# Taking over rooms for a latent attention stage one by one, with the last two projections side by side

## The chip, the cores and the metric

The kernel runs on one core of one Trainium2 chip. The metric is device time of one execution in microseconds (us), lower being better: here the median of three runs. TensorE does the matrix products, VectorE and ScalarE take results out of its banks (PSUM) and split or scale them, GpSimd (POOL) does some sums, and SyncE (SP) issues most transfers between memory and the on-chip buffer (SBUF), in the order in which they stand in its queue.

## The reference

One layer of a streaming encoder over 592 token rows: 16 learned meta rows, 512 prompt frames and 64 sample frames (with 128 cached rows in front of the latter). Everything is float32.

```python
z = rmsnorm(x, g) @ w_in                      # 8 differential heads (q, k, v), query latent 512, key latent 256, rotary key 64
cq = rmsnorm(cq_part, mla_q_norm_g)           # 4 blocks of 128: the "query latents"
qm = cq @ w_uq                                # per head 128 plain and 64 rotary columns
qm = concat(qm_plain, rope(qm_rot, pos))
ckv = rmsnorm(ckv_part, mla_kv_norm_g); krope = rope(kr_part, pos)
km, vm = expand_latent(ckv, w_ukv)            # per head 128 key and 128 value columns
sm = (qn . km + qr . krope) * MLA_SCALE       # 8 latent heads; softmax, times vm
x = x + concat(o_d, o_m) @ w_out              # o_d: 8 differential ("old") heads, o_m: 8 latent heads
x = x + (silu(h @ w_gate) * (h @ w_up)) @ w_down
```

`rope` turns the first and second half of 64 columns: `concat(x1*cos - x2*sin, x1*sin + x2*cos)`. The outputs hold the new keys, values, latents and rotated keys too.

## The kernel before

Activations lie transposed, 128 features on the partitions and the tokens along the row: 592 columns (`T`), 576 without the meta rows (`TQ`), 720 with the cached rows (`TP`). A float32 product is made of three products of rounded parts: an operand is split into a high part (ScalarE, `AF.Copy`) and a low part (VectorE, the subtract), and `mm3` (line 200) multiplies wh by xh, wh by xl and wl by xh, each in two halves of the columns.

The first stage (the block from line 333) holds x split into 16 rooms of high and low parts (`xh`, `xl`, pool `xp`). `projections()` (662) makes the 24 projections of the differential heads, whose attention (`diff_attend`) runs interleaved with it, and then seven more of 128 columns each: the key latents 4 and 5, the rotary key 6 (64 columns, loaded twice to fill 128: `dup`), and the query latents 0 to 3. Each is 16 pieces of x by six matmuls. After the rotary key, `key_latent_norm()` takes its squares' sum with `sum_squares()` (306), whose matmuls against ones run in full float32. Each differential head's output is stored to `mspill[h]`.

The second stage (from line 721) has pools of its own, so it begins when the first stage is over: it loads the eight old heads back from `mspill` (line 729, seven through POOL's queue), cos, sin, the rotation matrix, the cached rows and both masks. `latents()` (790) turns the rotary key (`rope`, 777: a matmul with the matrix `rot`, then a product with sin and one with cos), transposes the cached rows, splits the latents, and takes the query latents' norm. `latent_rows()` (821) transposes the latents back for the outputs. `heads()` (981) does the eight latent heads: `rotary_queries` for each pair of heads, `queries_keys`, `pair_values`, and `latent_attend`, which stores to `mspill[8 + h]`. `mix_out()` (851) multiplies the old heads with the first half of w_out, 16 outputs of 8 by 6 matmuls, each output (`xo`) added to x and stored to `x1spill`.

TensorE's program order is made by `Streams` (50 to 97): generators with a rank each, and a clock that the matmuls advance; the ready one of lowest rank goes on. `mix_out` has rank 30, so its products fill in where nothing else is ready. On the other engines the order follows from the same run, with a scheduler's changes.

The third stage (from line 1148) does the second half of the out-projection: pool `ma` has three rooms `x`, into which the eight latent heads are loaded and split:

```python
m = ma.tile([P, TQ], F32, name="x", tag="x", bufs=3)
load(m, mspill[8 + h])
```

Then the FFN follows (lines 1138 and 1142), by far the longest part. A pool's first tiles wait for all that used the same ground before.

## Time and profile before

| | us |
|---|---|
| median of 3 runs | 2452.48 (2449.06 to 2455.5) |
| the profiled execution | 2450.92 |
| its span in the profile | 2449.1 |
| TensorE busy (matmul) | 2391.8, 98% |
| VectorE busy | 1778.9, 73% |
| ScalarE busy | 1161.0, 47% |
| GpSimd busy | 714.6, 29% |

The busy shares are averages over the three stages. TensorE's share says only that waits are short in all; where they are and what ends them must be looked for in the stretches around the change, which lie between 430 and 840 us.

### The profile page before, as it was taken

The page shows a single profiled execution, that of the slowest core. Times are in us where ns is not written, and L with a number is a line of the kernel's source. Part 1 is how long each engine was busy: PE and PEld are TensorE (multiplying, and loading weights), DVE is VectorE, ACT ScalarE, POOL GpSimd, SP SyncE. Part 2 cuts the span into 40 slices and gives each one's busy share as a digit, 9 for nine tenths or more (in the row PEclk, how much of TensorE's full clock was granted, in tenths as well). Part 3 has the DMA queues.
Part 4 walks back from the last instruction along what each step waited for, and adds up shares of the span by engine and source line. Part 5 has one row for each costly group of instructions (what it writes and reads, how often), then busy time and mean ns, then how long its engine had stood idle before and what let it go on. Part 6 is the DMA issues. An engine that isn't in the chain of part 4 may idle for free.

```text
span 2449.1 us, 44580 instructions
## 1 busy us (share of the span) xinstructions
PE 2391.8 (98%) x17607; PEld 2350.9 (96%) x17607; DVE 1778.9 (73%) x2815; ACT 1161.0 (47%) x2204; POOL 714.6 (29%) x553
## 2 busy tenths in 40 slices
PE   8999999989999999999999999999999999999998
PEld 7999999978999899999999999999999999999998
DVE  5665566556555588777888788888887988887874
ACT  5544544343444455445555554555554433333445
POOL 0000000000000144645645445445454322222223
PEclk9999999989999999999999999999999999999999
DMA  8432323243322553334434443443344875654332
GB/s 246 135 92 83 82 82 98 73 129 110 105 87 72 181 170 127 122 104 157 137 130 146 142 154 116 152 157 127 135 150 163 287 237 175 225 164 162 106 116 83
DMA packets 334864, 338.02 MB, mean 138 GB/s; under 512 B 24208, under 2 KB 278039, under 8 KB 334655
## 3 DMA queue, kind: packets, MB, share of 16 engines
q1 hardware_dynamic: 334094, 333.11, 42.7%
q8 instruction: 138, 2.26, 0.4%
q0 software_dynamic: 560, 2.06, 0.2%
q14 instruction: 72, 0.58, 0.1%
HBM read 265.20 MB, written 72.61 MB: 138 GB/s over the span
## 4 chain that ended last, share of the span: by engine, by line
PE 52%; DVE 1%; DMA 0%; issue 0%; POOL 0%; ACT 0%; DVEq 0%; POOLq 0%; SPq 0%
PE m L1138 33%; PE m L1142 17%; PE m L204 2%; DVE wl L124 0%; PE m L1521 0%; DMA raw<-in_ffn_w_down 0%; DVE b L124 0%; DMA b<-sumspill 0%; POOL ws L1107 0%; DVE ws L124 0%; PE m L1535 0%; DVE y L124 0%; ACT wh L124 0%; POOL b L1508 0%; DVE c L124 0%
## 5 line engine op out<-in xcount | busy, mean ns | idle before, releaser
L1138 PE MATMUL m<-b,wh 128*128 128x288 f32 x7168 | 1048.0, 295 | 5.8 <-ACT wh L124 2.9
L1138 PEld LDWEIGHTS m<-b,wh 128*128 128x128 f32 x7168 | 983.6, 188 | 8.5 <-issue 4.6
L1142 PE MATMUL m<-b,wl 128*128 128x288 f32 x3584 | 580.2, 297 | 1.7 <-DVE wl L124 1.5
L1107 POOL TENSOR_TENSOR ws<-raw 128x512 f32<-128x512 f32 (+1 forms) x258 | 373.4, 1457 | 543.4 <-DVE wl L124 263.0
L1142 PEld LDWEIGHTS m<-b,wl 128*128 128x128 f32 x3584 | 514.0, 189 | 3.0 <-DVE wl L124 3.0
L124 ACT ACTIVATE wh<-ws 128x512 fp32r<-128x512 f32 (+1 forms) x340 | 283.3, 846 | 389.9 <-PE m L1138 251.5
L124 DVE TENSOR_TENSOR wl<-ws,wh 128x512 fp32r<-128x512 f32 (+1 forms) x340 | 386.9, 1149 | 89.6 <-ACT wh L124 89.6
L124 ACT ACTIVATE wh<-raw 128x512 fp32r<-128x512 f32 x387 | 227.4, 620 | 288.1 <-PE m L1138 258.0
L124 DVE TENSOR_TENSOR wl<-raw,wh 128x512 fp32r<-128x512 f32 x387 | 358.4, 952 | 7.3 <-ACT wh L124 6.8
L107 PE MATMUL ps<-xh,wh 128*128 128x296 f32 (+1 forms) x960 | 218.8, 309 | 1.4 <-ACT wh L124 1.4
L107 PE MATMUL ps<-xl,wh 128*128 128x296 f32 (+1 forms) x960 | 210.3, 300 | 1.5 <-DVE xl L124 1.5
L107 PE MATMUL ps<-xh,wl 128*128 128x296 f32 (+1 forms) x960 | 209.3, 299 | 0.7 <-DVE wl L124 0.6
L124 DVE TENSOR_TENSOR y<-y,m 128x288 f32<-128x288 f32 x312 | 140.1, 451 | 88.3 <-PE m L1142 68.0
L124 DVE TENSOR_TENSOR ws<-ws,raw 128x512 f32<-128x512 f32 (+1 forms) x129 | 110.3, 857 | 80.3 <-POOL ws L1107 78.5
L107 PEld LDWEIGHTS ps<-xh,wh 128*128 128x128 f32 x960 | 156.6, 191 | 5.2 <-ACT wh L124 2.1
L107 PEld LDWEIGHTS ps<-xl,wh 128*128 128x128 f32 x960 | 157.2, 191 | 2.2 <-DVE xl L124 2.2
L107 PEld LDWEIGHTS ps<-xh,wl 128*128 128x128 f32 x960 | 156.9, 191 | 1.4 <-DVE wl L124 1.4
L124 DVE TENSOR_TENSOR wl<-wr,wh 128x1024 fp32r<-128x1024 f32 (+1 forms) x110 | 117.1, 1065 | 43.4 <-ACT wh L124 42.1
L124 ACT ACTIVATE wh<-wr 128x1024 fp32r<-128x1024 f32 (+1 forms) x110 | 102.4, 932 | 69.5 <-PE ps L107 41.8
L1326 POOL TENSOR_TENSOR c<-c,rb 128x576 f32<-128x576 f32 x44 | 70.7, 1609 | 168.2 <-ACT c L124 168.2
L591 POOL MEMSET bias<- 64x64 f32 x8 | 1.2, 145 | 373.6 <-DMA bias<-tsk 321.7
L124 ACT ACTIVATE parts<-c 128x1 fp32r<-128x1 f32 x252 | 81.2, 322 | 37.5 <-DVE c L124 31.8
(354 smaller groups left out, 3110.7 us busy)
## 6 DMA issues: line engine op xcount, KB each, us to landing
raw<-in_ffn_w_gate SPq DMA_DIRECT2D x44, 1024.0 KB, 5.9
raw<-in_ffn_w_up SPq DMA_DIRECT2D x44, 1024.0 KB, 6.1
raw<-in_ffn_w_down SPq DMA_DIRECT2D x39, 1024.0 KB, 5.6
partspill<-parts SPq DMA_DIRECT2D x126, 288.0 KB, 2.1
b<-partspill SPq DMA_DIRECT2D x126, 288.0 KB, 6.0
wr<-in_w_in SPq DMA_DIRECT2D x60, 512.0 KB, 4.0
wr<-in_w_out SPq DMA_DIRECT2D x16, 512.0 KB, 4.0
wr<-in_w_out SPq DMA_DIRECT2D x32, 256.0 KB, 3.3
```

The source lines that it names most:

```text
L107: self.tc.keep_in_program_order(self.pe.matmul(out, lhsT, rhs, start=start, stop=stop))
L124: ins = issue(*args, **kwargs)
L204: PE.matmul(outs[i], w, x[i], start=start and p == 0, stop=stop and p == 2)
L591: G.memset(bias[0:64, 464:528], -BIG)
L1107: engine.tensor_tensor(w[:, k:k + m, :], pick(xs), pick(ys), op=op)
L1138: PE.matmul(banks[p], wh[:, k, :], x, start=first and new and k == 0 and x is hi, stop=False, skip_group_check=not new)
L1142: PE.matmul(banks[p], wl[:, k, :], hi, start=False, stop=last and k == n - 1, skip_group_check=not new)
L1326: G.tensor_tensor(g[:, f, :], g[:, f, :], rb2, op=ALU.mult)
```

## The change

The second stage loses its own pools: its tiles go into rooms that the first stage gives up one after the other.

- The last two query latents (2 and 3) are projected side by side, from weights of 4 by 256 columns, so that each piece of x is used for both and then released (`release(kc)`). Rooms 0 to 6 take the old heads 0 to 6 (loaded by SP and split at once), room 7 the last one, which is split from its own tile and no longer stored; room 8 and 9 the head weights (`mw`), 10 cos and sin, 11 the norm and the turned key (later the heads' output `o32`), 12 and 13 the rotary queries with their mask, 14 and 15 the plain queries. The other tiles go into rooms of keys and values (`kv`).
- `rope` has no matmul: four VectorE instructions of 32 partitions multiply each quarter with its sign and with sin into its partner quarter.
- The rotary key is projected with high and low part of the weights side by side in one 128-column operand (`project_stacked`): four matmuls for each piece of x in place of six.
- `sum_squares` adds the squares on GpSimd and multiplies their sum with ones once: two matmuls for four; for the query latents two for eight.
- Both masks are copied early inside memory; the cached rows are loaded in the first stage.
- `mix_out` and `heads` are in the same run of `Streams` as the projections.

```diff
+    def project_stacked(ps, wsrc, xs):
...
+            split(w[:, :, 0:DH], w[:, :, DH:P], wr)
...
+                for j, x in enumerate(xs[kc]):
+                    for i, xi in enumerate(halves(x)):
+                        PE.matmul(ps[:, i, 0:n], w[:, k, :], xi, start=kc + j == 0, stop=kc + j == KC)
...
     def sum_squares(...)
+            if total is None:
+                total = sq
+            else:
+                G.tensor_tensor(total, total, sq, op=ALU.add)
...
+            if h < H - 1:
+                store(mspill[h], o32)
+            else:
+                yield [released[h]]
+                mixh[h], mixl[h] = (x_room(h, w, f"mx{w}{h}")[:, 0:TQ] for w in "hl")
+                split(mixh[h], mixl[h], o32)
...
+            ps = [pjt(), pjt()]
+            for g in range(4):
+                wh, wl = weights(w_in[g * 4 * P:(g + 1) * 4 * P, off:off + 2 * P].rearrange(
+                    "(k p) c -> p k c", p=P), 4, 2 * P)
+                for k in range(4):
+                    kc = 4 * g + k
+                    for j in range(2):
+                        c = slice(j * P, (j + 1) * P)
+                        mm3([ps[j][:, 0, 0:QH], ps[j][:, 1, 0:QH]], wh[:, k, c], wl[:, k, c],
+                            halves(xsq[kc][0]), halves(xsq[kc][1]), kc == 0, kc == KC - 1)
+                        yield 0
+                    release(kc)
...
+        def release(kc):
+            released[kc]["done"] = True
+            if kc < H - 1:
+                mixh[kc], mixl[kc] = (x_room(kc, w, f"mx{w}{kc}")[:, 0:TQ] for w in "hl")
+                load(f32(mixl[kc]), mspill[kc])
+                S.activation(mixh[kc], f32(mixl[kc]), AF.Copy)
+                V.tensor_tensor(mixl[kc], f32(mixl[kc]), f32(mixh[kc]), op=ALU.subtract)
+            elif kc == 10:
+                for w, name, src in (("h", "cos", c_cos), ("l", "sin", c_sin)):
+                    at_x[name] = x_room(kc, w, name, F32)
+                    load(at_x[name], src)
...
         def rope(dst, z):
-            for i in range(2):
-                PE.matmul(pr[:, i, 0:w], rot, z[:, i * w:(i + 1) * w], start=True, stop=True)
-            V.tensor_tensor(hv(t, n), ev(pr, w), hv(sin[:, c], n), op=ALU.mult)
+            for a in range(0, P, 32):
+                b = a ^ 32
+                V.scalar_tensor_tensor(t[b:b + 32, :], z[a:a + 32, :], sign[a:a + 32, :], at_x["sin"][a:a + 32, c],
+                                       op0=ALU.mult, op1=ALU.mult)
...
-            o32 = aq[0].tile([P, TQ], F32, name="o32", bufs=1)
+            o32 = x_room(11, "l", "o32", F32)[:, 0:TQ]
```

What moves shows in the order of the instructions. The first place is TensorE's program behind the last projection matmul (`ps<-xh,wl`; mxh and mxl are an old head's parts, wh and wl weights). Before:

```order
L107 MATMUL ps<-xh_108,wl 128x288 x2
L107 MATMUL pr<-zl_5306,rot 128x296 [waits DMAHW1_49,DVE_49,PE_49]
L107 MATMUL pr<-zl_5306,rot 128x296
L111 MATMUL pkr<-ident,rn 128x128 [waits DMAHW3_49,DMAHW2_49,DMAHW4_49,DMAHW1_49,DMAHW5_49,DMAHW0_49,DMAHW6_49,DVE_49,DMAHW7_49,Activation_49,Pool_49]
L111 MATMUL pkr<-ident,cn 128x128 [waits DMAHW0_49]
L111 MATMUL pkr<-ident,cn 128x128
L107 MATMUL ps<-mxh_5966,wh 128x288 [waits DVE_49,Activation_49]
L107 MATMUL ps<-mxh_5966,wh 128x288
```

With the change, behind nine such rows of the first three old heads (cqh is a query latent's high part, mw a head's weights, sqs the summed squares):

```order
L107 MATMUL ps<-mxh_5693,wl 128x288 x2
L111 MATMUL pkr<-ident,cache 128x128 [waits DMAHW1_49]
L111 MATMUL pkr<-ident,cache 128x128
L111 MATMUL pkr<-ident,cache 128x128 [waits DMAHW3_49,DMAHW2_49]
L107 MATMUL ps<-cqh_5444,mw 128x288 [waits DVE_49]
L107 MATMUL ps<-cqh_5444,mw 128x288
L107 MATMUL ps<-cql_5445,mw 128x288 x2
L107 MATMUL ps<-cqh_5444,mw 128x288 x2
L107 MATMUL ps<-cqh_5622,mw 128x288 x2
L107 MATMUL ps<-cql_5623,mw 128x288 x2
L107 MATMUL ps<-cqh_5622,mw 128x288 x2
L107 MATMUL pq<-sqs,ones 128x288 [waits Pool_49]
```

The rotation and the transposes of the cached rows no longer stand first; three products of old heads do (the first row here is the last of them), then the transposes, then the first head's query projection with the norm's sum inside it.

The second place is VectorE's queue, some 15 instructions behind the evacuation of the last two projections, with the change (xo is an output of the mix, `zq` the first rotary query, `v` and `rsq` the norm's steps):

```order
L124 TENSOR_SCALAR v<-pq 128x576 [waits PE_49,Pool_49]
L124 TENSOR_TENSOR kr<-kr,t 128x592 [waits DVE_49]
L124 TENSOR_TENSOR wl<-wr,wh 128x1024 [waits DMAHW4_49]
L124 TENSOR_TENSOR v<-v,rsq 128x576 [waits DVE_49,Activation_49]
L124 TENSOR_TENSOR rkl_6004<-kr,rkh 64x592 [waits Activation_49]
L124 TENSOR_TENSOR rkl_6005<-kr,rkh 64x592
L124 SCALAR_TENSOR_TENSOR v<-v,rsq 128x576 [waits DVE_49]
L124 TENSOR_TENSOR xo<-xo,ps 128x576 [waits DMAHW4_49,PE_49]
L124 SCALAR_TENSOR_TENSOR rsq<-v,rsq 128x576 [waits DVE_49]
L124 TENSOR_TENSOR mw<-mw 128x512 [waits DMAHW3_49,DMAHW2_49,DMAHW1_49]
L124 SCALAR_TENSOR_TENSOR zq<-ps,rsq 128x576 [waits DVE_49,Pool_49]
L124 TENSOR_TENSOR wl<-wr,wh 128x1024 [waits DMAHW2_49,Activation_49]
```

The four quarters of `t<-zl,sign,sin` (the rotary key) stand just ahead of these rows, those of zq just behind `wl`, and the evacuation of xo between the steps of the norm.

The third place is SP's queue at the end of the latent heads (x: the third stage's rooms; o: a head's output; numbers are the buffers'). Before:

```order
L124 DMA x1spill<-xo 128x576 [waits DMAHW7_49,DVE_49]
L124 DMA x<-mspill 128x576 [waits DMAHW2_49,DMAHW1_49,DMAHW3_49,PE_49,Pool_49]
L124 DMA x<-mspill 128x576 x2
L124 DMA wr<-in_w_out 128x4x128 x2
L124 DMA x<-mspill 128x576 [waits DMAHW3_49,DMAHW0_49,DVE_49]
L124 DMA raw<-in_ffn_w_gate 128x8x256
L124 DMA mspill<-o_9116 128x576 [waits Activation_49]
L124 DMA x<-mspill 128x576 [waits DMAHW4_49,DVE_49]
```

With the change:

```order
L124 DMA mspill<-o_8785 128x576 [waits DMAHW0_49,Activation_49]
L124 DMA x1spill<-xo 128x576 [waits DMAHW6_49,DMAHW1_49,DVE_49]
L124 DMA mspill<-o_9043 128x576 [waits Activation_49]
L124 DMA x<-mspill 128x576 [waits DMAHW2_49,DMAHW0_49,DMAHW3_49,PE_49,Pool_49]
L124 DMA x<-mspill 128x576 x2
L124 DMA wr<-in_w_out 128x4x128
L124 DMA wr<-in_w_out 128x4x128 [waits DMAHW7_49]
L124 DMA x<-mspill 128x576 [waits DMAHW3_49,DVE_49]
```

The store of the last head's output stood behind the first loads of x and of wr; now it stands ahead of all of them. The room of that output lies on ground that the third stage's rooms get.

## Rows read from the trace of the kernel before

**Rows 1.** The table of stretches: us, each engine's busy us and instructions, clock, DMA share, GB/s

```profile
430.00:534.60 104.60, 104.46 (x758) 101.28 (x756) 53.50 (x109) 37.20 (x70) 0.14 (x1) 1.00 0.27 73
534.60:553.00 18.40, 7.71 (x29) 6.24 (x30) 13.70 (x23) 11.37 (x21) 5.32 (x8) 0.63 0.89 286
...
840.00:2449.00 1609.00, 1591.33 (x11935) 1585.20 (x11934) 1288.77 (x1824) 779.19 (x1420) 696.31 (x509) 1.00 0.46 152
```

**Rows 2.** What TensorE waited for, 430 to 830: total us, times, longest

```profile
PE pkr L111 <- DMA kmsk<-c_kmask: 8.1, 1, 8.1
PE pr L107 <- DMA rot<-c_rot: 2.4, 1, 2.4
PE tp L111 <- DVE pk0l L124: 2.0, 2, 1.4
```

**Rows 3.** Timeline of TensorE at the end of the projections: start, us, instruction [idle before]

```profile
534.13 0.42 PE L107 MATMUL ps<-xh,wl 128*128 128x288 f32 x2
536.96 1.79 PE L107 MATMUL pr<-zl,rot 128*128 128x296 f32 x4 [2.41 <-DMA rot<-c_rot]
546.84 0.45 PE L111 MATMUL pkr<-ident,rn 128*128 128x128 f32 x1 [8.09 <-DMA kmsk<-c_kmask]
```

**Rows 4.** Timeline of TensorE, the first latent score

```profile
583.05 0.23 PE L107 MATMUL sp<-kmh,qnh 128*128 128x144 f32 x1
```

**Rows 5.** Timeline of TensorE at the end of the latent heads

```profile
822.51 0.40 PE L107 MATMUL po<-p5h,vl 80*128 80x64 f32 x1
823.27 0.82 PE L204 MATMUL m<-mh,wh 128*128 128x288 f32 x2 [0.36 <-issue]
...
833.05 0.42 PE L204 MATMUL m<-mh,wh 128*128 128x288 f32 x2
```

**Rows 6.** Timeline of TensorE: key projection pairs, a float32 sum

```profile
455.46 0.43 PE L107 MATMUL ps<-xh,wh 128*128 128x296 f32 x2
455.73 0.43 PE L107 MATMUL ps<-xl,wh 128*128 128x296 f32 x2
...
554.03 1.13 PE L107 MATMUL ps<-sq,ones 128*128 128x288 f32 x4
```

**Rows 7.** Instruction groups of VectorE, 430 to 815: busy us, mean ns, idle before

```profile
L124 DVE TENSOR_TENSOR xo<-xo,ps 128x576 f32<-128x576 f32 x16 | 12.0, 752 | 4.6 <-PE ps L107 4.3
...
L124 DVE COPY nn<-pn 128x320 f32<-128x320 f32 x4 | 1.9, 484 | 0.5 <-PE pn L111 0.5
```

**Rows 8.** Instruction groups of GpSimd, 430 to 815

```profile
L786 POOL TENSOR_TENSOR zr<-zq,cos 128x576 f32<-128x576 f32 x4 | 6.6, 1657 | 183.1 <-DVE zq L124 183.1
```

**Rows 9.** Table of stretches, around the two places

```profile
546.80:552.00 5.20, 5.16 (x21) 4.82 (x21) 4.75 (x11) 3.96 (x9) 0.00 (x0) 0.58 1.07 361
820.00:828.00 8.00, 6.96 (x31) 6.60 (x31) 3.71 (x7) 3.29 (x7) 0.00 (x0) 0.57 1.01 311
```

**Rows 10.** Timeline of VectorE: a pair of 592 columns, two halves of a head

```profile
537.06 1.46 DVE L124 TENSOR_TENSOR cl<-zl,ch 128x592 fp32r<-128x592 f32 x2
...
573.32 0.75 DVE L124 TENSOR_TENSOR rq0s<-zr,rq0m 64x576 fp32r<-64x576 f32 x1
574.11 0.75 DVE L124 TENSOR_TENSOR rq1s<-zr,rq1m 64x576 fp32r<-64x576 f32 x1
```

**Rows 11.** Timeline of SyncE's queue at the end of the latent heads

```profile
815.25 1.27 SPq L124 DMA_DIRECT2D x<-mspill  x3
...
823.20 0.34 SPq L124 DMA_DIRECT2D mspill<-o  x1
```

**Rows 12.** Timeline of ScalarE at the end of the latent heads

```profile
823.67 0.68 ACT L124 ACTIVATE mh<-x 128x576 fp32r<-128x576 f32 x1 [0.50 <-DMA x<-mspill]
```

**Rows 13.** DMA issues, 790 to 840 (KB each, median us to landing); then all mxl loads

```profile
x<-mspill SPq DMA_DIRECT2D x8, 288.0 KB, 3.4
...
x1spill<-xo SPq DMA_DIRECT2D x3, 288.0 KB, 2.1
...
DMA to landing us min/median/max: 2.8/6.8/8.6
```

More of the change, by code (lines that the diff above doesn't have):

```diff
@@ L304, in hv, with sum_squares @@
         return t[:, 0:n].rearrange("p (a b) -> p a b", a=2)
-    def sum_squares(pq, tiles, tile_of):
-        for n, z in enumerate(tiles):
-            w = z.shape[1] // 2
-            sq = tile_of("sq")[:, 0:2 * w]
-            S.activation(sq, z, AF.Square)
-            yield 1.2
-            for i in range(2):
-                PE.matmul(pq[:, i, 0:w], ones, sq[:, i * w:(i + 1) * w],
-                          start=(n == 0), stop=(n == len(tiles) - 1))
+    PSUMS = {}
+    def sum_squares(bank, tiles, tile_of):
+        n = tiles[0].shape[1]
+        total = None
+        for z in tiles:
+            sq = tile_of("sq")[:, 0:n]
+            S.activation(sq, z, AF.Square)
+            yield 0.8
+            if total is None:
+                total = sq
+            else:
+                G.tensor_tensor(total, total, sq, op=ALU.add)
+        yield 1.8
+        yield from st.take(bank)
+        pq = PSUMS[bank]()
+        for i in range(2):
+            PE.matmul(pq[:, i, 0:n // 2], ones, total[:, i * (n // 2):(i + 1) * (n // 2)], start=True, stop=True)
+        return pq
     xspill = dp.tile([KC, P, TQ], F32, name="xspill")
@@ new lines, in projections, with query_columns @@
+            yield [scored[H - 1]]
+            for j, z in enumerate([query_columns(p) for p in ps]):
+                query_latent(2 + j, z)
+            for j in range(2):
+                st.give("ps", 1.5)
+            st.spawn(2, latent_keys(), [att[H - 1]])
+            normed.append(st.spawn(0, query_norm()))
+            st.spawn(20, heads())
+            st.spawn(30, mix_out())
+        cqh, cql = [None] * 4, [None] * 4
+        sqs = [None, None]
+        normed = []
+        def query_columns(ps):
+            z = ztile()[:, 0:TQ]
+            V.tensor_tensor(hv(z, TQ), ev(ps, QH), hv(rb[:, NM:T], TQ), op=ALU.mult)
+            return z
@@ L777, in rope, with query_norm @@
+        def query_norm():
+            yield 5.0
+            yield from st.take("sp")
+            pq = sbig("pq")
+            for i in range(2):
+                PE.matmul(pq[:, i, 0:QH], ones, sqs[0][:, i * QH:(i + 1) * QH], start=True, stop=True)
+            v = ztile("v")[:, 0:TQ]
+            V.tensor_scalar(hv(v, TQ), ev(pq, QH), 1.0 / QL, EPS, op0=ALU.mult, op1=ALU.add)
+            st.give("sp", 1.5)
+            rsqrt(at_x["rsq"], v)
         def rope(dst, z):
             n = z.shape[1]
-            w, c = n // 2, slice(T - n, T)
@@ L780, in rope @@
[L780 to L792 removed]
+            c = slice(T - n, T)
@@ new lines, in latent_keys @@
+        def latent_keys():
+            rkh = keys_room("kh0", "rkh")
+            rkl = [keys_room("kh1", "rkl0"), keys_room("kl", "rkl1")]
+            ch.extend([keys_room("kh0", "ch0"), keys_room("kh1", "ch1")])
+            cl.extend([keys_room("kl", "cl0"), values_room("vh", "cl1").rearrange("p a b -> p (a b)")[:, 0:TP]])
+            rk.extend([rkh, rkl])
+            cache = ap.tile([P, 4, P], F32, name="cache", tag="na")
+            load(cache[:, 0:2, :], cache_ckv.rearrange("p (a c) -> p a c", a=2))
+            for r in both:
+                load(cache[:, 2, r], cache_kr)
+            for i in range(2):
+                oth = slice(64 - i * 64, 128 - i * 64)
+                load(f32(rkl[i][oth, :]), kmask[oth, :])
@@ L809, in latents @@
-            st.give("tp", 4.0)
-            for i in range(4):
-                split_scaled(cqh[i], cql[i], zs[i], gq[:, i:i + 1])
-            yield from st.take("ps")
-            pq = pjt()
-            yield from sum_squares(pq, zs[0:4], ztile)
-            v = ztile("v")[:, 0:TQ]
-            V.tensor_scalar(hv(v, TQ), ev(pq, QH), 1.0 / QL, EPS, op0=ALU.mult, op1=ALU.add)
-            rsqrt(rsq, v)
-            st.give("ps", 1.5)
+                sub_lo(rkl[i][both[i], 0:T], kr[both[i], :], rkh[both[i], 0:T])
@@ L994, in heads @@
                     if j:
-                        yield [att[h - 1]]
+                        yield [lat[h - 1]]
                     yield from pair_values(j)
-        first = st.spawn(0, latents())
-        rows = st.spawn(1, latent_rows(), [first])
-        st.spawn(20, heads(), [first])
-        st.spawn(30, mix_out())
+        for name, n in (("ps", 0), ("sp", 0), ("tp", 1), ("po", 1)):
+            st.bank(name, n)
+        st.spawn(9, projections())
         st.run()
@@ L1637, in shape_constants @@
     cos, sin = np.cos(ang).astype(np.float32), np.sin(ang).astype(np.float32)
-    rot = np.zeros((P, P), np.float32)
+    rot = np.ones((P, 1), np.float32)
     for base in (0, 64):
-        for i in range(half):
-            rot[base + half + i, base + i] = -1.0
-            rot[base + i, base + half + i] = 1.0
+        rot[base + half:base + 64] = -1.0
     km = np.zeros((P, TP), np.float32)
```

266 lines of the change are left out of this document (139 added, 127 removed).

## The prediction

> **What bounds the kernel now.** I read the kernel by stages first: the table of stretches [rows 1] gives TensorE's busy time and granted clock between fixed times. From 840 us to the end, which the change does not touch, TensorE is busy for 1591.33 of 1609 us, and in the projections (430 to 534.6) for 104.46 of 104.6. Nothing waits there, so a matmul saved in the projections is its whole time saved. The hole is 534.6 to 553: 7.71 us of work in 18.4, at a mean clock of 0.63. The list of what TensorE waited for [rows 2] names it: 8.1 us for the key mask and 2.4 us for the rotation matrix, both loaded by DMA. The timeline [rows 3] shows them in order: the last projection matmul at 534.13, the rotation at 536.96, the first transpose of the cache at 546.84, behind which the products of the old heads begin. So the first question is what fills that hole. Two more places count: the first latent score at 583.05 [rows 4], up to which everything is a chain of small products, and the end of the latent heads, where the last product with the values starts at 822.51 and the next stage's first product at 823.27 [rows 5], with only 0.36 us between.
>
> The profiled execution took 2450.92 us (a span of 2449.1), 1.56 below the median of the three runs; the sum is made against 2450.92, and 1.56 is added at the end. About 0.3%, 7.4 us, is what a measurement of this kernel can tell from no change.
>
> **1. Up to the last projection matmul.** The rotary key's 96 matmuls of 296 columns become 64. A pair starts 0.27 us after the pair before it, both column halves together [rows 6], so one is 0.134 us, and 32 fewer give -4.3. The key latent's sum of squares loses one of its two float32 pairs; such a pair takes 1.13 us as listed, and 0.97 when the start of the next product inside it is taken off [rows 6]: -1.0. The two query latents side by side are the same matmuls in another order. Two new waits stand against that: latent 1's bank is evacuated late behind the attention of the last old head (0.3), and an old head's subtract on VectorE stands ahead of an attention split while its load, issued only when its room of x is released, lands in about 3 us (0.4). Sum -4.6. The bounds are -5.3 without new waits and about -2 if every one of the seven old heads' loads costs 0.4.
>
> **2. From there to the first latent score.** Now that is 534.4 to 583.05, 48.65 us. Of it about 31.4 is TensorE's own work, counted by matmuls: 102 mix matmuls and 48 of the query projections at 0.1325 (pairs 0.26 to 0.27 apart, [rows 3, 6]), 12 of 360 columns, four sums of squares and two rotations at 0.97, transposes. The change takes out three sums (-2.9) and both rotations (-2.0) and does six mix matmuls more (+0.8): 27.3 us. What is left is the waiting. The masks now go straight into their rooms long before, so the 8.1 and 2.4 us [rows 2] are gone; what is late next is VectorE. By the order, VectorE has some 45 instructions from the evacuation of the two side-by-side latents to the first key split, 34 us by their durations [rows 7]: about 0.75 us for everything of 576 columns, 0.48 for each of five copies of rows, the weight splits longer; the four quarters of a rotation do not get cheaper by having 32 partitions, since 64 partitions take as long (0.75, [rows 10]) as 128 (0.752, [rows 7]). So one rotation costs VectorE 3.0 us in place of 0.75, which the matmul's removal on TensorE pays for only where VectorE is not awaited. Walking that queue against TensorE's I get these waits: 0.85 for the two evacuations behind the last old head's norm; 1.95 for the query norm's sum, behind two adds on GpSimd at 1.66 each (the nearest row is its multiply of the same shape, 1.657 [rows 8]); 1.85 for the second mix output's bank, whose evacuation (xo) stands behind the first rotation; 1.8 for the copies of rows behind the second rotation; 1.7 for two banks of the mix; 1.1 for zn; 0.35 for an xo load; 1.4 for a weight split of the first head. Together 11.0. With them go 1.1 us for a clock that falls once in such a patchy stretch (the row of 546.8 to 552 shows 0.58 where TensorE was busy for 5.16 of 5.2 us [rows 9], so about 2 us lost in that spell; half of it is taken). 27.3 + 11.0 + 1.1 = 39.4, so -9.2. The low end is VectorE never waiting for anything, 36 us (-12.6); the high end is as patchy as now, 48.65 (0).
>
> The quarters start in changing groups of 32 partitions. Two subtracts of one head's halves, which start in different groups, stand 0.79 us apart at 0.75 each, while a pair of equal ones takes 1.46 for two of 0.77 [rows 10]: the overlap of 0.08 is missing in the first case. The Trainium skill has this as a rule (VectorE: DVE Perf Modes, Two Vector instructions with no wait between them): an instruction whose input or output starts in another quadrant than the one before is held until all earlier Vector instructions have finished. By it the eight quarters of this stretch lose their overlap, some 0.6 us in all by the rows, which I leave inside the 11.0.
>
> **3. From the first score to the last product with the values.** Three rotations on TensorE go (-2.9), six mix matmuls were done earlier (-0.8), the rotations' extra 2.25 us each on VectorE delay an evacuation here and there (+0.5). The mix now ends before the last head does, where about 30 of its matmuls (4 us) lie behind the last scores today. The transposes there already wait for VectorE's splits, 2.0 us in two waits for the first piece alone [rows 2]; I give one more such wait, +1.0. Sum -2.2; bounds -3.7 and +0.3 (all cover lost).
>
> **4. The boundary to the second half of the out-projection.** Its x rooms lie now on ground that the last head's output room holds, so the order puts the loads of x behind the store of that output, and the first of them waits for it. Today three loads are issued at 815.25, and the store only at 823.20 [rows 11]. After the change: last product 822.51, copied out by 823.2 as now, the store issued there and landed 2.1 us later as the stores of this size do on quiet queues (the stores of x1 [rows 13]), 825.3. Eight x tiles go through three rooms, so three rounds of a load (L) and of copy and subtract (0.68 and 0.75, [rows 7, 12]), and the last heads' products 1.6: the first output ends at 825.3 + 3(L + 1.43) + 1.6 = 831.2 + 3L. It ends at about 833.0 now [rows 5], so the loss is 3L - 1.8. L is 3.4 as median of these loads now, among a weight load of 1 MB, and 2.8 for a load of that size by itself (the least of the old heads' loads) [rows 13]; the 1 MB load stands behind them after the change, so I take 3.0: +7.3. The weights of that stage, issued behind three loads, land at about 830 and are not later than x. Bounds +6.6 (2.8) and +18.6 (6.8, the median of old heads' loads when many were under way at once [rows 13]).
>
> **Sum:** -4.6 - 9.2 - 2.2 + 7.3 = -8.7: 2442.2 for a profiled execution, **2443.8** as a median of runs.
>
> **Rivals.**
> - *More is gained* (0.17). VectorE's queue is never what TensorE waits for, the low end of part 2 (-12.6) with L at 2.8: -4.6 - 12.6 - 2.2 + 6.6 = -12.8, 2439.7. For it: today's waits for VectorE are short [rows 2]. Against it: 34 us of VectorE's work before the first score, in order.
> - *The rotation by quarters makes VectorE the bound* (0.18). Each of its some twelve hand-overs with ScalarE or GpSimd is exposed by 0.7 more and the wait for it stands in TensorE: part 2 gives 0, the sum is +0.5, 2453. For it: 34 us against 27.3 of matmuls; against it: the order puts other work between most of them.
> - *The clock stays low* (0.08). Two stretches lie near the half level of 1.2 GHz: 546.8 to 552 (0.58) behind 8 us in which TensorE stood idle, and 820 to 828 (0.57) behind short waits, with 6.96 of 8 us busy [rows 9]. A spell of 7 us there costs about 3; two more of them in the patchy stretch and one after the boundary give +6 to +7 on the sum, 2450. The Trainium skill (TensorE: Matmul & The Clock Gate, HAM oscillation) describes this for kernels that alternate short bursts of matmuls with waits for DMA: the clock falls again in each wait. The second stretch agrees in part: the waits of the engine ahead of it were of 0.7 us only.
> - *Slower: the boundary in three rounds of slow loads* (0.06). At L of 8.6, the longest seen for such a load [rows 13], the boundary costs 24.0 and the sum is +8.0: 2460.5. It decides from L of about 8.4. For it: all loads of that stage now start at once behind one store. Against it: only three x loads are in flight at a time.
> - *The change doesn't fill the hole* (0.03), since mix products wait for loads that start only when x rooms are released: part 2 at 0 and part 1 at -2, sum +3, 2456.
>
> **How the numbers follow.** My forecast has 0.48. It is the case of faster by a little over 0.3% at 2443.8 (the limit is 2445.1), and its own error is some 4 us to each side, so 0.3 of that 0.48 is faster and 0.18 the same. With the 0.17 faster is 0.47. No change takes the 0.18 and the cases at 2450 to 2456, 0.47 together. Slower is 0.06. The range 2436.5 to 2454.5 holds the forecast, the larger gain, and the cases at 2450 and 2453; left out are the slower case, the unfilled hole and what lies below.
>
> **What would show it.** TensorE's wait for masks and rotation gone, and in its place several waits of 1 to 2 us that name VectorE or GpSimd; the first latent score about 14 us earlier, near 569; at the end of the latent heads one gap of 7 to 8 us before the first m product, with x or wr by DMA as releaser, and the first output ending about 9 to 10 us after x landed. The sum is wrong if the gap there is under 4 or over 12 us, or if the first score comes after 575.

## The result, and the profile after

The median of 20 runs is 2457.18 us (2453.22 to 2462.16) against 2452.32 for 20 runs of the kernel before on the same chip (2448.57 to 2456.97): a ratio of 1.002, with a 95% interval of 1.0013 to 1.0027. The change makes the kernel 4.9 us slower; by the bound of 0.3% that is no change, by the interval it is a small loss. The forecast was 2443.8, faster. It was wrong in sign, and the time lies outside the range.

The profiled execution of the kernel after took 2460.72 us (a span of 2458.9). It is 3.5 above its own median, and that of before was 1.4 below the median of these 20, so the two traces lie 9.8 apart where the medians lie 4.9 apart. Cut at the same five events, they compare like this (us):

| stretch | before | after | forecast | measured |
|---|---|---|---|---|
| start to the sixth old head's norm sum | 412.8 | 413.5 | 0 | +0.7 |
| to the last projection matmul | 121.4 | 119.4 | -4.6 | -2.0 |
| to the first latent score | 48.8 | 47.1 | -9.2 | -1.6 |
| to the last product with the values | 239.5 | 240.1 | -2.2 | +0.6 |
| to the 49th matmul of the third stage, its first output | 10.5 | 19.8 | +7.3 | +9.3 |
| to the last matmul | 1606.9 | 1609.6 | 0 | +2.7 |

The first and the last row are code that the change does not touch. In the profiles of the experiments below, the last row is between 1602.9 and 1609.1; what it differs by here says nothing. All four rows of the change came out 2.0 to 7.6 us worse than forecast.

What TensorE waits for between 532 and 580 us, in the trace after (us in total, times, longest):

```profile
PE pn L111 <- DVE nn L124: 4.3, 3, 3.0
PE pq L107 <- POOL sqs L808: 2.7, 1, 2.7
PE ps L107 <- DVE xo L124: 2.1, 1, 2.1
PE pv L107 <- DVE mw L124: 1.5, 1, 1.5
PE ps L107 <- DVE zn L124: 0.9, 1, 0.9
PE ps L107 <- DVE z L124: 0.8, 1, 0.8
```

The waits for the mask and the rotation matrix [rows 2] are gone, as forecast; six rows stand there now, eight waits and 12.3 us in all, and five of the rows name VectorE. The table of stretches, with the columns of [rows 1]:

```profile
430.00:532.80 102.80, 100.44 (x725) 96.85 (x724) 62.03 (x121) 45.86 (x85) 5.58 (x4) 1.00 0.38 109
532.80:541.20 8.40, 4.95 (x38) 4.52 (x36) 8.37 (x11) 4.77 (x8) 3.66 (x2) 0.99 0.14 37
541.20:545.00 3.80, 3.80 (x13) 3.23 (x14) 3.68 (x7) 0.28 (x1) 0.00 (x0) 0.57 0.00 0
545.00:561.00 16.00, 10.90 (x78) 9.96 (x77) 14.98 (x20) 4.76 (x7) 2.34 (x1) 1.00 0.40 119
561.00:572.00 11.00, 9.74 (x41) 8.20 (x42) 4.59 (x7) 2.46 (x4) 1.21 (x10) 0.53 0.46 125
572.00:580.00 8.00, 5.52 (x37) 4.92 (x36) 4.08 (x7) 2.78 (x5) 0.00 (x0) 1.00 0.35 105
810.00:820.50 10.50, 9.11 (x32) 6.24 (x30) 2.10 (x4) 2.45 (x5) 0.00 (x0) 0.53 0.00 0
820.50:830.30 9.80, 0.04 (x1) 0.03 (x1) 2.25 (x4) 2.88 (x5) 0.00 (x0) 0.50 0.70 222
830.30:834.70 4.40, 4.40 (x19) 4.40 (x20) 3.50 (x5) 2.68 (x4) 0.00 (x0) 0.51 0.74 215
```

The third busy number is VectorE's. From 532.8 to 561 it is busy for 8.37, 3.68 and 14.98 us, 27.0 of 28.2: there it is the bound, and TensorE has 19.7 of work. From 561 to 580 it is the other way round: VectorE is idle for 10.3 of 19 us. Its longest idle time there ends where TensorE's query projection ends, which ran at the half level of the clock (TensorE's row, then VectorE's; zn is the scaled projection, and the DMA that the view names is the last semaphore to come by the profile, not the last operand):

```profile
572.38 0.43 PE L107 MATMUL ps<-cqh,mw 128*128 128x288 f32 x2
572.85 0.76 DVE L124 SCALAR_TENSOR_TENSOR zn<-ps,rsq 128x576 f32<-128x576 f32 x1 [4.83 <-DMA xo<-xspill]
```

The clock falls twice in this stretch, to 0.57 and 0.53, that is near the 1.2 GHz level, each time behind a wait of about 3 us, and the second time it stays low from 561 to 572, with TensorE busy for 9.74 of these 11 us. At the end of the heads it falls at 811, ten microseconds earlier than before the change [rows 9], and stays low until 834.7.

The boundary, in TensorE's timeline (answers to [rows 5]) and in SyncE's queue (to [rows 11]):

```profile
820.14 0.40 PE L107 MATMUL po<-p5h,vl 80*128 80x64 f32 x1
830.30 0.82 PE L199 MATMUL m<-mh,wh 128*128 128x288 f32 x2 [9.77 <-DMA x<-mspill]
```

```profile
820.82 0.32 SPq L124 DMA_DIRECT2D mspill<-o  x1
823.04 1.27 SPq L124 DMA_DIRECT2D x<-mspill  x3
824.36 0.98 SPq L124 DMA_DIRECT2D wr<-in_w_out  x2
```

The chain is the one forecast: the store at 820.82, the loads of x 2.2 us behind it, when it has landed. What the first output then waits for are the three rounds of x. Here are the second and third round's issues, the copies on ScalarE that wait for each round (the row of wh in between is the weights'), and TensorE's wait for the third:

```profile
827.50 3.04 SPq L124 DMA_DIRECT2D x<-mspill  x3
832.65 1.08 SPq L124 DMA_DIRECT2D x<-mspill  x2
```

```profile
825.99 1.35 ACT L124 ACTIVATE mh<-x 128x576 fp32r<-128x576 f32 x2 [5.19 <-DMA x<-mspill]
829.58 0.63 ACT L124 ACTIVATE wh<-wr 128x512 fp32r<-128x512 f32 x1 [0.18 <-DMA wr<-in_w_out]
831.14 1.42 ACT L124 ACTIVATE mh<-x 128x576 fp32r<-128x576 f32 x2
837.14 1.42 ACT L124 ACTIVATE mh<-x 128x576 fp32r<-128x576 f32 x2 [1.09 <-DMA x<-mspill]
```

```profile
837.87 0.67 PE L199 MATMUL m<-mh,wh 128*128 128x288 f32 x3 [0.64 <-ACT mh L124]
```

### The profile page after: what moved, and what is told of

The parts are those of the page before. It is cut to its first block, busy times and chain, and to the rows that moved or that the text cites. A ratio compares the mean times of both kernels' runs of the same rounds, so it can differ in the third digit from the quotient of the medians.

```text
span 2458.9 us, 44446 instructions
## 1 busy us (share of the span) xinstructions
PE 2384.6 (97%) x17539; PEld 2343.2 (95%) x17539; DVE 1801.3 (73%) x2828; ACT 1162.6 (47%) x2205; POOL 717.9 (29%) x550
## 4 chain that ended last, share of the span: by engine, by line
PE 65%; DVE 4%; DMA 2%; POOL 1%; issue 1%; ACT 1%; DVEq 0%; POOLq 0%; ACTq 0%; SPq 0%
PE m L1234 35%; PE m L1238 18%; PE m L199 5%; PE ps L107 4%; DVE wl L124 1%; PE po L107 1%; PE sp L107 1%; DVE b L124 1%; DMA raw<-in_ffn_w_down 1%; PE tp L111 1%; POOL ws L1203 1%; DMA raw<-in_ffn_w_gate 1%; DMA raw<-in_ffn_w_up 1%; PE pv L107 1%; DMA x<-mspill 0%
## 5 line engine op out<-in xcount | busy, mean ns | idle before, releaser
L124 ACT ACTIVATE wh<-ws 128x512 fp32r<-128x512 f32 (+1 forms) x340 | 283.4, 845 | 386.6 <-PE m L1234 242.0
L107 PE MATMUL ps<-xh,wl 128*128 128x296 f32 (+1 forms) x928 | 201.7, 299 | 0.1
L107 PEld LDWEIGHTS ps<-xh,wl 128*128 128x128 f32 x928 | 150.7, 189 | 0.8 <-DVE wl L124 0.8
```

The source lines that it names most:

```text
L107: self.tc.keep_in_program_order(self.pe.matmul(out, lhsT, rhs, start=start, stop=stop))
L124: ins = issue(*args, **kwargs)
```

## The experiments

Theory A after these readings: two causes take the expected gain. VectorE's queue sets the stretch up to the first latent score, and the store of the last output sets the boundary. Rivals: the clock's half level is the cause of the first, or GpSimd's sums are; and slow loads are the cause of the second. What cost the other two stretches (2.6 and 2.8 us worse than forecast) had no experiment of its own beyond e6, e10 and e11. Each chip ran the kernel before beside the experiments; its median there was 2451.85 (first four), 2451.63 (next four), 2451.74 (e10, e11) and 2453.61 (e13, e14). "The stretch" is always that from the last projection matmul to the first latent score.

### e1: the last output outside the rooms of x

```diff
-            o32 = x_room(11, "l", "o32", F32)[:, 0:TQ]
+            o32 = ztile("o32")[:, 0:TQ] if h == H - 1 else x_room(11, "l", "o32", F32)[:, 0:TQ]
```

> The last latent head's output goes to a tile outside the rooms of x, all else as in the change; SP's order then has the store of that output behind the loads of x again. Theory A (the gap before the out-projection's second half is only the store that the loads wait for): the 9.8 us wait before the first m product falls under 2 us, the first output of that stage ends 8 to 9 us earlier relative to the last product with the values, and the time is about 8 us under the change's, near 2449. Rival B (the loads are slow there anyway, or the 1 MB weight load that stands among them again delays x): at least half of the gap stays, gain under 4 us.

Measured: 2448.17, 9.0 under the change's median; against before 0.9985 (0.9976 to 0.9993). The boundary in TensorE's timeline and in SyncE's queue:

```profile
824.32 0.40 PE L107 MATMUL po<-p5h,vl 80*128 80x64 f32 x1
825.08 0.82 PE L199 MATMUL m<-mh,wh 128*128 128x288 f32 x2 [0.36 <-issue]
```

```profile
810.00 1.28 SPq L124 DMA_DIRECT2D x<-mspill  x3
811.32 0.98 SPq L124 DMA_DIRECT2D wr<-in_w_out  x2
...
825.00 0.32 SPq L124 DMA_DIRECT2D mspill<-o  x1
```

The loads go out 15 us ahead of the store, and the 9.8 us are 0.36; the first output ends 9.4 us behind the last product with the values, in place of 19.8. Theory A holds for the boundary, with its whole price; the 1 MB weight load that stands among the loads again (rival B) costs nothing that shows. This alone makes the change a gain of 3.7 us against the kernel before.

e1 also gives a yardstick for the experiments below. In the stretch, TensorE, VectorE, ScalarE and GpSimd each have the same instructions in the same order as in the change, and yet it is 45.3 here in place of 47.1 (columns as in [rows 1]):

```profile
537.00:582.30 45.30, 32.43 (x199) 29.16 (x198) 35.58 (x49) 14.95 (x24) 7.19 (x13) 0.92 0.34 98
```

VectorE is as busy as in the change (35.7), but the mean clock is 0.92, not 0.86, and the stretch is 1.8 shorter. So a difference of up to 2 us between two traces of this stretch says nothing by itself, and a difference in the clock can be a part of a larger one.

### e2: the copies of rows on ScalarE

```diff
-                V.tensor_copy(nn[0:n, 0:320], pn[0:n, 0:320])
+                S.activation(nn[0:n, 0:320], pn[0:n, 0:320], AF.Copy)
```

> The five copies of the latents' rows go from VectorE to ScalarE, all else as in the change, TensorE's order the same. Theory A (the copies behind the rotation's quarters in VectorE's queue make the 3.0 us gap and two of 0.6, and the clock's half level that follows it): the gap shrinks under 1 us, the clock stays high from 557 to 572, and the first latent score comes 7 to 9 us earlier, near 572; time about 2449. Theory B (VectorE's total work is the bound): the waits move to zn and the splits behind, the first score at most 2 us earlier.

Measured: 2455.73 (1.0012, 1.0001 to 1.0022), the stretch 43.8, 3.3 less than in the change and 1.5 less than in e1. The longest of these waits fell from 3.0 to 0.9 us, but there are four now, 3.0 in all. Between the two theories: at most half of what A wanted in the stretch, and in the medians 1.5 us, which the intervals don't tell from nothing.

### e3: three sums on TensorE

```diff
-                G.tensor_tensor(sqs[0], sqs[0], z, op=ALU.add)
+                if i == 1:
+                    G.tensor_tensor(sqs[0], sqs[0], z, op=ALU.add)
+                else:
+                    squared.append(z)
...
+                for n, t in enumerate([sqs[0]] + squared):
+                    PE.matmul(pq[:, i, 0:QH], ones, t[:, i * QH:(i + 1) * QH], start=n == 0, stop=n == len(squared))
```

> The squares of query latents 2 and 3 are summed by TensorE again (three float32 pairs in place of one); latents 0 and 1 are still added on GpSimd, all else as in the change. Theory A (the norm's sum waits for GpSimd's two adds, 2.7 us, and the clock falls in that wait): the wait falls under 0.5 us, the spell of half clock at 541 to 544 goes, TensorE does 1.9 us more, the first score 2 to 3 us earlier. Theory B (VectorE's queue is what counts, the sum only fills time): the score comes at the same time within 1 us or later.

Measured: 2456.64 (1.0019, 1.0008 to 1.003); the stretch 43.7, 3.5 less than in the change (1.7 less than in e1, at the same clock of 0.92) although TensorE does about 1.9 us more; the wait for the sum is no longer in the list, and the clock is 1.00 from 541 to 545. The wait for the copies of rows grew from 4.3 to 6.6 us, and VectorE is busy for 33.6 in place of 35.7, since the two of its instructions that met GpSimd's adds in the change, of 1.77 and 1.85 us, take 0.75 and 0.83 (last section). A gain as in theory A is there in the stretch, hardly above the yardstick; in the medians of the whole it does not show (the change's own ratio is 1.002).

### e5: TensorE kept busy in the two longest waits

```diff
+        def keep_busy(count):
+            now = st.now
+            po = pso.tile([P, 512], F32, name="busy", tag="po")
+            for n in range(count):
+                PE.matmul(po[:, 0:QH], cqh[0][:, 0:P], cqh[0][:, 0:QH], start=True, stop=True)
+            st.now = now
...
             yield from st.take("sp")
+            keep_busy(18)
...
+                if j == 1:
+                    keep_busy(22)
                 pn = tbank("pn")
```

> 40 products that nothing reads are put into the two longest waits of the stretch (18 ahead of the norm's sum, 22 ahead of the second copy of rows), 5.3 us of TensorE at full clock, all else as in the change. Theory A (of the stretch's excess over its 27 us of work some 6 us is TensorE at half clock behind those two waits): the clock stays near 1.0 from 541 to 545 and from 561 to 572, and the first latent score comes 3 to 6 us earlier in spite of the added products. Theory B (the stretch is as long as VectorE's queue): the clock may stay high, but the waits behind grow and the score moves by under 1.5 us.

Measured, in a single execution: 2457.55, the stretch 47.7. TensorE's timeline there (only rows with added products or waits):

```profile
541.17 2.53 PE L107 MATMUL busy<-cqh 128*128 128x288 f32 x18
544.07 1.24 PE L107 MATMUL pq<-sqs,ones 128*128 128x288 f32 x4 [0.37 <-POOL sqs L808]
555.09 0.85 PE L107 MATMUL ps<-mxh,wh 128*128 128x288 f32 x2 [4.21 <-DVE xo L124]
```

The clock stays at 1.00 behind the sum (541 to 547.5), as wanted, and TensorE reaches the next bank earlier; there it waits 4.2 us for xo in place of 2.1. What the clock gives back, the wait for VectorE takes. The half level was lifted only in the first place: it came at 555 instead, behind that wait (0.66 up to 563), and again behind 570 (0.87 up to 583). Over the whole stretch the clock is 0.89 in place of 0.86, TensorE has the added products to do, and VectorE's order changed by a few instructions. So this shows how one wait takes what another gives back; the price of the clock it does not measure.

### e6 and e7: the rotation with fewer VectorE instructions

e6 brings back the matmul with the rotation matrix (and so ten float32 matmuls):

```diff
-            for a in range(0, P, 32):
-                b = a ^ 32
-                V.scalar_tensor_tensor(t[b:b + 32, :], z[a:a + 32, :], sign[a:a + 32, :], at_x["sin"][a:a + 32, c],
-                                       op0=ALU.mult, op1=ALU.mult)
+            yield from st.take("sp")
+            pr = sbig("pr")
+            for i in range(2):
+                PE.matmul(pr[:, i, 0:w], rot, z[:, i * w:(i + 1) * w], start=True, stop=True)
+            V.tensor_tensor(hv(t, n), ev(pr, w), hv(at_x["sin"][:, c], n), op=ALU.mult)
```

> The rotation is a matmul with the rotation matrix again and one VectorE product, all else as in the change (ten float32 matmuls more, 1 us per pair; per rotation three VectorE instructions of 0.75 fewer). Theory A (VectorE's queue sets the stretch between the last projection and the first latent score): the stretch gets shorter, 47.1 to about 44, although TensorE has 2 us more to do in it; from the first score to the last product with the values at most 2 us longer; time 2455 to 2457. Theory B (TensorE's work and the clock set it, the quarters are covered): the stretch is 2 us longer, and the time 4 to 5 us above the change's.

Measured: 2456.39 (1.0018, 1.0009 to 1.0027). The stretch 41.7, 5.4 less than in the change (3.6 less than in e1); from the first score to the last product 241.8, 1.7 more. e7 keeps the matmul out and lets ScalarE move the quarters:

```diff
-                V.scalar_tensor_tensor(t[b:b + 32, :], z[a:a + 32, :], sign[a:a + 32, :], at_x["sin"][a:a + 32, c],
-                                       op0=ALU.mult, op1=ALU.mult)
+                S.activation(t[b:b + 32, :], z[a:a + 32, :], AF.Copy, scale=sign[a:a + 32, :])
+            V.tensor_tensor(t, t, at_x["sin"][:, c], op=ALU.mult)
```

> ScalarE, which is busy for a third of that stretch, moves the four quarters with their signs, and VectorE multiplies by sin once for all 128 partitions; no matmul for the rotation, all else as in the change. Theory A (VectorE's queue): 4.5 us of VectorE's work leave the stretch, which falls from 47.1 by 3 to 5 us; time 2452 to 2454. Theory B (clock and GpSimd's sum set it): under 1.5 us.

Measured: 2449.89 (0.9999, 0.9989 to 1.0008), 7.3 under the change's median. The stretch 41.1, 6.0 less (4.2 less than in e1). The stretch as one row, of the change and then of e7 (columns as in [rows 1]):

```profile
532.90:580.10 47.20, 34.91 (x200) 30.83 (x199) 35.71 (x49) 15.04 (x24) 7.21 (x13) 0.86 0.33 94
```

```profile
536.80:578.00 41.20, 32.44 (x200) 28.99 (x199) 29.34 (x43) 21.29 (x32) 7.12 (x13) 0.92 0.37 108
```

VectorE is busy for 6.4 us less and the stretch is 6.0 shorter; ScalarE does 6.2 more, and TensorE has no wait for it in this stretch's list that the change did not have. The clock rises too, from 0.86 to 0.92, but e1 has that clock with VectorE at 35.6, and is 4.2 longer than e7. So theory A is shown, with one limit: relieving VectorE is worth about 4 us of this stretch at an equal clock, and some 2 us of the 6.0 can be the clock's. e6 says the same the other way round: TensorE has about 2 us more to do, VectorE 6.7 less (28.97), the clock is 0.92, and the stretch is 5.4 shorter than in the change.

### e8 and e9: the repairs together

e8 is e1, e2 and e7 in one; e9 has e3 too.

> The output outside the rooms of x, the copies of rows on ScalarE and the quarters on ScalarE together. If VectorE's queue and the boundary are the two causes, their gains add up: the gap before the first m product under 2 us (-9), the stretch up to the first score at 40 to 42 in place of 47.1; time about 2442 to 2444, under both kernels. If relieving VectorE only moves the waits to GpSimd's sum and the loads, the time is that of the first experiment, 2447 to 2448.

> As the run before, and the squares of query latents 2 and 3 summed by TensorE again. With VectorE relieved the wait of 2.7 us for GpSimd's adds counts: the stretch 1 to 2 us shorter than in the run before, time 2441 to 2443. If it does not count, equal within 1 us or 1 us later, by the float32 products added.

Measured: e8 2442.07 (0.9959, 0.9945 to 0.9973), the stretch 41.0. e9 2439.35 (0.9951, 0.9939 to 0.9964), the stretch 38.5, its row here:

```profile
535.60:574.10 38.50, 32.56 (x207) 28.96 (x206) 25.68 (x38) 23.24 (x37) 3.45 (x11) 0.96 0.39 115
```

The two causes add up, nearly: e1 is 9.0 and e7 7.3 under the change, and e8 is 15.1 under it. The copies of rows add nothing to this in the stretch (41.1 in e7, 41.0 in e8), though VectorE is busy for 2 us less. With VectorE relieved, the wait for GpSimd's adds was 4.0 us in e7 and e8, and giving the sums back to TensorE is worth 2.5 us of the stretch, with the clock at 0.96 in place of 0.92; in the medians it is 2.7, and the intervals of the two overlap. Both are faster than both kernels: e9 by 12.3 us than the kernel before.

### e10: the mix held back; e11: the rotary key by six matmuls

e10 has e9's edits and `yield [asked[H - 1]]` ahead of the last output of the mix; e11 has e9's edits and the old projection of the rotary key.

> The four edits of the run before (2439.35), and the last output of the mix is held until the last latent head's scores are through, so that its 48 matmuls stand among that head's transposes and products. Theory A (the missing cover at the end of the heads costs waits for VectorE and lets the clock fall, 8 to 9 us at the half level before the last product): the clock stays at 1.0 there, the stretch from the last scores to the last product gets longer by less than the 6.4 us that the 48 matmuls leave earlier; the time is 2 to 3 us lower. Theory B (the products are worth as much where they stood, among the scores): within 1.5 us, or later because the loads of x now wait for the mix.

Measured: 2440.22 (0.9951, 0.9939 to 0.9964), no different from e9. The clock is at 1.00 in the last 10 us of the heads, where e9 has 0.50, but it lies at 0.50 from 791 to 797.6 instead. The heads are 1.7 us shorter, no more than e1 and the change differ in that stretch (242.0 and 240.1); the gap at the boundary is 2.3 in place of 0.8, with a load of x as releaser, and the next 400 matmuls take 4 us longer. That is theory B: moving the half level gains nothing in all. That the later loads are what took the gain back is a reading, not tried by itself.

> The four edits of e9 (2439.35), with the rotary key projected by six matmuls for each piece of x again, both halves of the weights loaded twice. Theory A (nothing waits in that stretch, so 32 matmuls cost their own time): 4 to 4.5 us above e9, near 2443.6, and 4.3 us more between the sum of head 6 and the last projection matmul. Theory B (the attention of the old heads beside it has waits that the shorter projection only brings to light): 1 to 2.5 us.

Measured: 2443.86 (0.9969, 0.9958 to 0.9981), 4.5 above e9; the stretch up to the last projection matmul 124.2 against 119.3. Theory A: the 32 matmuls are worth their whole time. The edit also brings back the larger weight split and the simpler evacuation of the old projection; what these are worth was not tried apart.

### e13 and e14: the product with cos on VectorE

```diff
-            G.tensor_tensor(dst, z, at_x["cos"][:, c], op=ALU.mult)
+            V.tensor_tensor(dst, z, at_x["cos"][:, c], op=ALU.mult)
```

> The rotation's product with cos goes from GpSimd to VectorE, all else as in the change, TensorE's order the same. Theory A (the first quarter of a rotation takes 1.4 to 1.9 us in place of 0.81 because it can't run beside GpSimd's product, which reads the same buffer): the first quarter of all four query rotations takes 0.81, that of the key's rotation, which runs beside GpSimd's two adds of squares, stays at 1.8; VectorE gains 1.0 and loses 0.75 per rotation, so the time stays within 2 us of the change's. Theory B (a first quarter is slow by itself, by the change of partitions ahead of it): 1.4 to 1.9 us stay.

Measured: 2455.80 (1.0012, 1.0003 to 1.0021), the stretch 44.9, within the yardstick (45.3 in e1). VectorE's rows of the quarters in the trace of the change, and those of e13 (mean ns is the last number ahead of the idle time):

```profile
L124 DVE SCALAR_TENSOR_TENSOR t<-zq,sign,sin 32x576 f32<-32x576 f32 x16 | 15.6, 974 | 0.4
L124 DVE SCALAR_TENSOR_TENSOR t<-zl,sign,sin 32x592 f32<-32x592 f32 x4 | 4.3, 1083 | 0.1
```

```profile
L124 DVE SCALAR_TENSOR_TENSOR t<-zq,sign,sin 32x576 f32<-32x576 f32 x16 | 13.0, 810 | 0.4
L124 DVE SCALAR_TENSOR_TENSOR t<-zl,sign,sin 32x592 f32<-32x592 f32 x4 | 4.3, 1082 | 0.1
```

The query rotations' quarters fall to 0.81 each; those of the key, whose first one runs beside GpSimd's adds, keep their mean. Theory A is shown; for the time of the kernel nothing follows.

> The four edits of e9 (2439.35) and the product with cos on VectorE. There the quarters are on ScalarE, so VectorE is idle while they run, and its product with cos stands in that time. Theory A: the rotations' chains get 0.9 us shorter each and nothing on VectorE is held by GpSimd's product; 0 to 2 us under e9. Theory B (VectorE's queue is still full there): 0.5 to 1 us above e9.

Measured: 2439.28 (0.9942, 0.9929 to 0.9956), as e9 to a tenth; against the kernel before, which was slower beside it, 14.3 us less in place of 12.3, with intervals that overlap. The stretch is 38.6. Neither theory's gain or loss can be told from nothing here.

## Why the prediction was wrong

- **Part 1, the projections (-4.6, measured -2.0).** The term of the rotary key is right: e11 gives 4.9 in the trace and 4.5 in the medians for the -4.3. The new waits were mis-sized: 0.7 in the sum, 2.4 in the list for this stretch (1.1 for a split of the last old head's attention, 1.3 for scores), and by e11's stretch (124.2 against 121.4, with 1.0 saved on the key's sum) the side-by-side projection costs 3.8. The mechanism of the largest is the one named, as VectorE's timeline shows:

```profile
510.25 0.76 DVE L124 TENSOR_TENSOR mxl<-mxl,mxh 128x576 fp32r<-128x576 f32 x1 [0.44 <-ACT mxh L124]
510.93 0.68 DVE L124 TENSOR_TENSOR pk0l<-tp,pk0h 128x512 fp32r<-128x512 f32 x1
```

  The subtract of an old head stands ahead of the split and waits for its own copy; the split (pk0l) is what TensorE waits 1.1 us for. What makes up the rest of the 3.8 was not tried.

- **Part 2, up to the first score (-9.2, measured -1.6).** This is the step that failed: the overlap of TensorE's work with VectorE's queue, and the clock's term with it. The sum had 27.3 of work, 11.0 of waits and 1.1 for the clock, 39.4. The trace has 34.9 busy and 12.3 of waits, 47.2. Of the 7.6 more in the busy time about 6 are the clock (an estimate: 3.8 us busy at 0.57 and 9.7 at 0.53, so 1.6 + 4.6) and the rest is work that the count missed. The waits' sum came out near, in part by luck: the copies of rows took 4.3 and not 1.8, while 2.05 put on banks of the mix and on an xo load are not in the list. The prediction had named the sign for this: a first score after 575; it came at 580.06.

  Behind the waits is the rival that I gave 0.18, VectorE as the bound: it priced this part at 0, which is nearer than -9.2. VectorE's queue was put at 34 us and taken as covered but for 11; it was busy for 35.7, and up to 561 it had 1.2 us to spare. From 561 on TensorE at the half level is what VectorE waits for, as the rows above show. How the two share the loss can be told from e1 and e7 alone, with one trace each: at a clock of 0.92 in place of 0.86 and VectorE as busy as in the change the stretch is 1.8 shorter (e1); at the same 0.92 with VectorE's 6.4 us gone it is 4.2 shorter again (e7). Over all the traces the stretch goes with VectorE's busy time in it: 47.2 for 35.7, 44.9 for 35.4 (e13), 43.8 for 33.4 (e2), 41.7 for 29.0 (e6), 41.2 for 29.3 (e7), 38.5 for 25.7 (e9), 38.8 for 24.3 (e11), from 9.5 to 14.5 us more. But as VectorE's time falls the clock rises, from 0.86 to 0.96, so these numbers alone do not part the two. The kernel before had the same 35.8 in 48.8: the change took away the loads' wait and left the queue behind it as long as it was.

- **The quarters were mis-priced too.** They were put at 0.75 each. They take 0.81, and the first of a rotation 1.4 to 1.9 where it runs beside a GpSimd instruction (below). A rotation cost VectorE 3.2 to 4.3, not 3.0. The trace agrees with the rule on quadrants that the prediction weighed: four quarters one behind the other stand 0.82 apart in e13 (3.28 for four at 0.81), without overlap.

- **Part 3, the heads (-2.2, measured +0.6).** Three rotations' matmuls were put at 2.9; bringing them back costs this stretch 1.7 (e6), no more than two executions differ here: e1, whose edit touches this stretch only at its end, has 242.0 where the change has 240.1. The lost cover was taken at 1.0. The clock falls to the half level at 811 there, which nothing in the sum held; e10 shows only that moving it with the mix's products gains nothing in all. What cost the 2.8 stays open.

- **Part 4, the boundary (+7.3, measured +9.3).** The mechanism was right and e1 shows it whole. The size was off in one term, the load L, taken at 3.0: by the rows above, the three rounds took 2.9, 3.6 and 4.5 us from their issue to the copy that waited for them (823.04 to 825.99, 827.50 to 831.14, 832.65 to 837.14), 2.1 more than three times 3.0, which is the whole excess. The weights, said to be "not later than x", do set the first product, which came 10.2 behind the last one with the values: their copy (829.58) ended at 830.21. But the end of the first output is set by the third round, for which TensorE waits again at 837.87. (At L = 3.0 the prediction's formula gives +7.2, not +7.3.)

- **The rivals.** The chances were not sound. Rivals that worsen the sum were weighed one by one, as if only one of them could hold. VectorE's bound and the falls of the clock came together, and the range did not hold that; that a queue with no slack is the cause of both, and of the waits in the projections too, is my reading. One row was also read short: ahead of the fall at 820 in the kernel before, TensorE waited 1.4, 0.7 and 0.7 us (the 1.4 is in [rows 2]), not 0.7 alone.

## What to carry to other kernels

When a wait on a load is taken away, add up the busy time of the engine that stands next in line over the same stretch. If it is nearly as long as the stretch without the wait, little is won, and what the change adds to that engine counts: here four instructions for one, and taking them off it again shortened the stretch by 4 to 6 us. Compare the granted clock of two traces before a difference is given to the edit. Before a room is shared, look at which transfer the next owner's first load will wait for: here moving one tile of the last head was worth 9 us, more than any arithmetic in the change.

## What the hardware showed that was not expected

In these traces a VectorE instruction with two operands in SBUF does not run beside a GpSimd instruction that reads SBUF and began first: the quarters end only some 0.6 us after that one has ended. The first quarters of the query rotations, with GpSimd's product beside them, in the trace of the change (VectorE, then GpSimd):

```profile
554.66 4.34 DVE L124 SCALAR_TENSOR_TENSOR t<-zq,sign,sin 32x576 f32<-32x576 f32 x4
...
741.96 1.81 DVE L124 SCALAR_TENSOR_TENSOR t<-zq,sign,sin 32x576 f32<-32x576 f32 x1
```

```profile
553.58 2.34 POOL L855 TENSOR_TENSOR zr<-zq,cos 128x576 f32<-128x576 f32 x1 [12.44 <-DVE zq L124]
...
741.49 1.67 POOL L855 TENSOR_TENSOR zr<-zq,cos 128x576 f32<-128x576 f32 x1 [60.38 <-ACT e L124]
```

GpSimd ends at 743.16, the quarter at 743.77; its normal time is 0.81, and it took 1.81. In the second rotation, where GpSimd's product ended before the quarters began, the first took 0.81 as the others did, and in e13, without that product, all four of each did. The third stage of the same trace shows the condition: 126 of VectorE's splits (wl<-raw,wh of 128x512, both operands in SBUF) began while GpSimd worked and took 1.47 us as median in place of 0.68 alone; 92 of its sums with an operand in a bank (c<-c,m of 128x288) began so too and took 0.45, as alone. The Trainium skill states it (SBUF — State Buffer, SBUF: two separate sides): VectorE and GpSimd share one pair of ports, and whichever starts first holds it for its whole instruction. The trace agrees, with 0.6 to 1.0 us lost by each of these quarters; and the first of the two products on GpSimd, which began inside a split on VectorE (553.41 to 554.63), took 2.34 where the other took 1.67. The prediction did not weigh this rule, although the change moves sums to GpSimd beside a full VectorE; the adds of squares held the key's first quarter in the same way (1.85), and the subtract of the last old head ahead of it (1.77 in place of 0.75).
